# Fixed order for the routing of the last two token tiles in a one-core encoder layer with 16 experts

## The chip, the core and the metric

One core of a Trainium2 chip runs the whole layer in one launch. The metric is the device time of that launch in microseconds (us), lower is better. The core has five instruction streams that run beside each other and wait for each other through semaphores: TensorE (PE in the profile; PEld is its weight load), VectorE (DVE), ScalarE (ACT), GpSimd (POOL) and SyncE (SP), of which the last only issues DMAs here. Each stream runs its own instructions strictly in the order in which the program has them.

## What is computed

512 tokens of width 1024 pass one layer. An input LayerNorm, one combined projection, three mixers beside each other (differential attention, a gated delta rule, a diagonal state-space model) and one output projection give the residual stream, which a second LayerNorm (ln1) normalises. Then comes a mixture of 16 experts and a last LayerNorm. The change stands where ln1 and the routing are:

```python
h = layer_norm(ALPHA * h + mix, ln1_g, ln1_b)
g_prob = softmax(h @ w_grp + b_grp); g_p, g_idx = top_k(g_prob, 1)
e_sel  = the 4 expert logits of that group
e_val, e_idx = top_k(e_sel, 2); e_w = softmax(e_val) * g_p
for e in range(16):
    hid = silu(h @ w1[e]) * (h @ w3[e])
    out += comb[:, e] * (hid @ w2[e])      # comb: 0 unless e was chosen
h = layer_norm(ALPHA * h + out, ln2_g, ln2_b)
```

All is float32; products are split into a high and a low part where needed (`e_hi`, `e_lo`, `w_hi`, `w_lo`).

## The kernel before, in words

**The stage before the experts.** The tokens stand in four tiles of 128. For tile t the generator `out_t(t)` (L1306) is the whole chain from the output projection to the routing: it loads the residual tile `xo`, adds the output projection in three groups of input blocks and two halves of 512 columns (matmuls into `pA`, one VectorE addition each), takes `bn_stats` of the last sum of each half, transposes the half (L1331, four transposes into `pG`, copied to `xT` by ScalarE), computes the 24 router logits from `xT` (`pl`, sixteen small matmuls), finishes the LayerNorm statistics (`ln_end`, a chain of small VectorE operations with Ln and Exp on ScalarE), and forms the logits row `lg` (tile `oblk` in the profile). Then it normalises `xo` with two `scalar_tensor_tensor` operations (L1348 and L1349) and writes it to the arrays `hdr` and `yd` in memory through GpSimd's DMA queue (L1354, L1355). Then the routing proper (L1357 to L1385): `max`, `max_index`, mask, `max`, `max_index`, the two 0/1 rows `o0`, `o1` and their sum `mb`; a small matmul with a triangular matrix counts the tokens ahead (`pr_`) and gives the slot row `sv`. From `sv`, `one_hot` (L212) makes 0/1 matrices `oh` (token by slot) for experts 0 and 1, 2 to 7 and 8 to 15, in three VectorE operations.

**From routing to experts.** The last tile's first `oh` is followed by `slot_rows` (L217): eight tiny matmuls over all four tiles and two small VectorE operations give the table `tab` of the token numbers of experts 0 and 1, which GpSimd needs to gather their tokens from `hdr` into `xg` (L1495). `weights_all` (L1402) computes the gate weights of all tiles into `aux`; `slot_all` (L247) multiplies all `oh` by `aux` with 64 small matmuls (`pS`), and only behind them TensorE's order has `turn_x`, the transposes of the gathered tokens with which expert 0 begins.

**What sets the order.** Instructions inside a `tc.manual_schedule()` block keep the order of the program on each engine. `weights_all`, `slot_all`, and everything of the experts are in such blocks. All before them is ordered by the framework's scheduler: it takes from the program order what it holds to be ready, so the order of `ORDER2` (L37), a list of how many steps of which generator come next, is a priority, and tiles interleave freely on VectorE. The helper `run(g, n)` (L366) advances a generator by n steps.

**The experts.** The weights of 16 experts come in 192 loads of 512 KB (`e_raw`, L1632, on SyncE's queue) into a ring of 32 buffers. The first 28 go as soon as the memory of the earlier stage is free. Load 29 (`FIRST = 28`, L1633) waits by hand for the first two gathers to have landed. Every later load waits for a buffer of the ring, that is for VectorE to have split it or TensorE to have used it. From expert 3 on the order of the experts depends on the token counts (`rank_all`, L255).

Of the kernel before, what the change touches and what calls it, by code (L numbers as in the profile page):

```python
# [15 lines left out]
AF = mybir.ActivationFunctionType  # L16
ALU = mybir.AluOpType
# [4 lines left out]
P = 128  # L22
D = 1024
S = 512
NT = S // P
# [10 lines left out]
          "G11 V1 g2 h G11 S1 G23 G12 S1 V0 G22 S1 G21 V2 G01")  # L36
ORDER2 = ("q00 R3 q01 R1 q10 R4 q11 A01 q20 R1 A02 O11 A01 R1 A02 O01 A03 q21 A01 W2 A11 W2 A01 R1 A11 O01 A12 "  # L37
# [3 lines left out]
NQ4 = 4  # L41
RING = (2, 8, 15, 14, 21, 13, 12, 11, 9, 10, 29, 7, 30, 18, 31, 16, 17, 19, 20, 27, 28, 0, 1, 4, 5, 22, 23, 24, 25, 26, 3, 6)
OHT = 20
# [6 lines left out]
AHEAD = 0  # L50
SW = 12
POOL = 4
NORM = 'vvvv'
KG = ((3, 7, 0, 1), (2, 4, 5), (6,))
FIRST = 28
POOLE = ()
# [23 lines left out]
def tile_layer(ctx: ExitStack, tc: tile.TileContext, a, out):  # L80
    nc = tc.nc

    def tt(o, x, y, op, e=nc.vector):
        return e.tensor_tensor(o, x, y, op=op)  # L84
# [6 lines left out]
    def stt(o, x, s, y, op0, op1):  # L91
        return nc.vector.scalar_tensor_tensor(o, x, s, y, op0=op0, op1=op1)  # L92

    def act(o, x, f, **kw):
        return nc.scalar.activation(o, x, f, **kw)  # L95
# [45 lines left out]
    ident = ones_tile([P, P], "ident")  # L141
# [67 lines left out]
    hdr = dram.tile([S, D], F32, name="hdr")  # L209
    yd = dram.tile([S, D], F32, name="yd_")  # L210
# [6 lines left out]
    def slot_rows(oh, e0, e1, p):  # L217

        p = p[:, 0:2 * (e1 - e0)].rearrange("p (e c) -> p e c", c=2)
        for e in range(e0, e1):  # L220
            for t in range(NT):
                mm(p[:, e - e0], oh[t][e // 8][:, :, e % 8], AXS[t][:, e, 0:2], t == 0, t == NT - 1)
        nc.vector.tensor_reduce(tab[1][:, e0:e1], p, axis=AX.X, op=ALU.add)
        ts(tab[0][:, e0:e1], tab[1][:, e0:e1], 4096.0, ALU.add)
# [133 lines left out]
    gp, ve = nc.gpsimd, nc.vector  # L358
# [7 lines left out]
    def run(g, n=1):  # L366

        for _ in range(n):
            next(g, None)

    with ExitStack() as t1:
        wv = t1.enter_context(tc.tile_pool(name="wv", bufs=1))
# [15 lines left out]
        psA, psG, psT = banks(A=2, G=4, T=2)  # L388

        def per(name, dt=F32, shape=None):  # L390
            return wr.tile(shape or [P, S], dt, name=name, tag="per", bufs=15)
# [50 lines left out]
        for t in range(NT):  # L442
            x = f4("x")
# [3 lines left out]
        for t0 in range(0, NT, LNB):  # L447
# [6 lines left out]
            r = sm.tile([P, LNB], F32, name="ln_rb")  # L454
            rsqrt(r, mv[:, :, 1], LNB, sm, LN_EPS)
            for j in range(LNB):
                x = xs[t0 + j]
# [3 lines left out]
        for k in range(KT):  # L461
            p = psT()
# [17 lines left out]
        beta, g, eg, ek = g6("beta"), g6("g"), g6("eg"), g6("ek")  # L480
# [598 lines left out]
        psA, psG, psT, psV = banks(A=4, G=2, T=1, V=1)  # L1079
# [191 lines left out]
        g1 = []  # L1271
# [27 lines left out]
        MB, OH = [], {}  # L1299
# [3 lines left out]
        TOP = b16[:, 0:64].rearrange("p (t x c) -> p t x c", t=NT, x=2)  # L1303
        O2 = o16.rearrange("p (t x c) -> p t x c", t=NT, x=2)

        def out_t(t):  # L1306
            x = q4k("xo")
            gp.dma_start(x, h0d[t * P:(t + 1) * P, :])
            yield 1
            st_ = sm.tile([P, 2, 6], F32, name="ln_st")  # L1310
            xT = [per("xT"), per("xT")]
            for g_ in KG:
                for n in range(2):
                    c = slice(n * 512, n * 512 + 512)
                    x_ = x[:, c]
                    p = psA()
                    for k in g_:
                        while (k, t) not in yT:
                            run(R if k < 3 else AA[k - 4])
                        while k not in wo:  # L1320
                            run(WO)
                        mm3(p, yT[k, t], [w[:, c] for w in wo[k]], k == g_[0], k == g_[-1])
                    if g_ == KG[0]:
                        stt(x_, x_, ALPHA, p, ALU.mult, ALU.add)
                    else:
                        tt(x_, x_, p, ALU.add)
                    if g_ == KG[-1]:
                        nc.vector.bn_stats(st_[:, n, :], x_)
                        p = psG()
                        for j in range(4):  # L1330
                            nc.tensor.transpose(p[:, j * P:(j + 1) * P], x_[:, j * P:(j + 1) * P], ident)  # L1331
                        act(xT[n], p, AF.Copy)
                    yield 1

            if not g1:
                route_init()
            pl = psG()
            for k in range(KT):
                mm(pl[:, 0:24], xT[k // 4][:, (k % 4) * P:(k % 4 + 1) * P], rw24[:, k, :], k == 0, k == KT - 1)
            mu, r = ln_end(st_, sm)  # L1340
            nmr = sm.tile([P, 1], F32, name="nmr")
            stt(nmr, mu, -1.0, r, ALU.mult, ALU.mult)
            lg = LG[:, t]
            stt(lg, cs24, nmr, rowb, ALU.mult, ALU.add)
            stt(lg, pl[:, 0:24], r, lg, ALU.mult, ALU.add)
            yield 1
            if NORM[t] == "v":
                stt(x, x, mu, g1[0], ALU.subtract, ALU.mult)  # L1348
                stt(x, x, r, g1[1], ALU.mult, ALU.add)  # L1349
            else:  # L1350
                act(x, x, AF.Identity, scale=r, bias=nmr)
                tt(x, x, g1[0], ALU.mult, e=gp if NORM[t] == "p" else ve)
                tt(x, x, g1[1], ALU.add, e=gp)
            gp.dma_start(hdr[t * P:(t + 1) * P, :], x)  # L1354
            gp.dma_start(yd[t * P:(t + 1) * P, :], x)  # L1355
            yield 1
            m8, m8e = TOP[:, t, 0], TOP[:, t, 1]  # L1357
            ix = sm.tile([P, 8], U32, name="ix")
            nc.vector.max(m8, lg[:, 0:8])
            nc.vector.max_index(ix, m8, lg[:, 0:8])  # L1360
            gi = sm.tile([P, 1], F32, name="gi")
            nc.vector.tensor_copy(gi, ix[:, 0:1])
            em = sm.tile([P, 16], F32, name="em")
            ts(em, giq, gi, ALU.not_equal, NEG, ALU.mult)
            tt(em, em, lg[:, 8:24], ALU.add)
            ixe = sm.tile([P, 8], U32, name="ixe")
            nc.vector.max(m8e, em)
            nc.vector.max_index(ixe, m8e, em)
            ei = sm.tile([P, 2], F32, name="ei")
            nc.vector.tensor_copy(ei, ixe[:, 0:2])  # L1370
            o0, o1 = O2[:, t, 0], O2[:, t, 1]
            ts(o0, i16, ei[:, 0:1], ALU.is_equal)
            ts(o1, i16, ei[:, 1:2], ALU.is_equal)
            while len(MB) < t:
                run(OT[len(MB)])
            mb = const.tile([P, 16], BF16, name="mb%d" % t)
            tt(mb, o0, o1, ALU.add)
            MB.append(mb)

            pr_ = psG()  # L1380
            mm(pr_[:, 0:16], oneb, o64, True, False)
            for t_ in range(t):
                mm(pr_[:, 0:16], oneb, MB[t_], False, False)
            mm(pr_[:, 0:16], strib, mb, False, True)
            sv = const.tile([P, 16], BF16, name="sv%d" % t)  # L1385
            stt(sv, mb, -8192.0, pr_[:, 0:16], ALU.mult, ALU.add)
            SV.append(sv)
            yield 1
            oh = [per("oh", BF16, [P, P, 8]) for i in range(2)]
            for i, e0, e1 in ((0, 0, 2), (0, 2, 8), (1, 0, 8)):  # L1390
                one_hot(oh[i][:, :, e0:e1], sv[:, 8 * i + e0:8 * i + e1])
                if t == NT - 1 and e1 == 2:
                    for t_ in range(t):
                        while t_ not in OH:
                            run(OT[t_])
                    OH[t] = oh
                    slot_rows(OH, 0, 2, psT())
            if t < NT - 1:
                OH[t] = oh
            yield 1  # L1400

        def weights_all():  # L1402
# [32 lines left out]
        R, AA, WO = recur(), [attend(i) for i in range(3)], wout()  # L1435
        OT = [out_t(t) for t in range(NT)]
        streams = {"R": R, "W": WO}
        for x in ORDER2.split():
# [9 lines left out]
                run(AA[int(x[1])], int(x[2:]))  # L1448
            else:
                run(streams[x[0]], int(x[1:]))  # L1450
        for x in AA + OT:
            run(x, 20)
        with tc.manual_schedule():
            weights_all()
            pst.close()
            t2 = ctx.enter_context(ExitStack())
            ps2 = t2.enter_context(tc.tile_pool(name="ps2", bufs=1, space=PSUM, reuse_waits="tile"))
            PS = [ps2.tile([P, 512], F32, name="pS", tag="S%d" % i) for i in range(2)]
            CT = PS[1][:, 128:144]
            for t in range(NT):  # L1460
                mm(CT, oneb, MB[t], t == 0, t == NT - 1)
            SA = slot_all(OH, PS[0])
# [8 lines left out]
    def psT():  # L1471
        return ps2.tile([P, 512], F32, name="pT", tag="T", bufs=2)
# [257 lines left out]
    with tc.manual_schedule():  # L1730
# [138 lines left out]
        for x, op in ((0, ALU.mult), (1, ALU.add)):  # L1869
            for c in range(2):  # L1870
                x_ = xs[1][:, half(c)]
# [15 lines left out]
    with tc.If(more > P):  # L1887
        for e in (NE - 2, NE - 1):
            scatter(xgs[e % 2][:, 0:512], at(0, e), 2)
        for r in range(0, S // P):  # L1890
            oh = []
            for t in range(NT):
                p = psT()
# [8 lines left out]
                o = traw().bitcast(BF16).rearrange("p (i s e) -> p i s e", i=2, e=8)  # L1902
# [100 lines left out]
```

## Time and profile before

| | us |
|---|---|
| median of three runs | 780.49 |
| lowest and highest of them | 778.73, 789.08 |
| the profiled execution | 780.58 |
| its span, first to last instruction | 778.8 |
| busy: PE, PEld, DVE, ACT, POOL | 685.2, 497.0, 522.7, 352.5, 101.5 |

The rows further down are from that one profiled execution; their times count from the span's start, and 1.8 us of the execution lie outside the span. A timeline row has the start, the duration, the engine, the line, the operation, its result and inputs, and in brackets the idle time before it with what ended it. A line can be that of a helper: L84 is `tensor_tensor`, L92 `scalar_tensor_tensor`, L95 ScalarE's `activation`, L101 `matmul`.

### The profile page before, as it was taken

How to read it: one execution, taken by the hardware profiler on the slowest of the kernel's cores; microseconds unless marked ns; L12 is line 12 of the kernel's file. 1: busy time of each engine (PE TensorE's matmuls, PEld its weight loads, DVE VectorE, ACT ScalarE, POOL GpSimd, SP SyncE). 2: the span in 40 equal slices, each digit the busy share in tenths (PEclk: the TensorE clock that was granted, in tenths of full speed). 3: DMA queues.
4: the chain of work that ended last, by engine and by line, in shares of the span. 5: the costliest groups of instructions: out<-in, count | busy, mean ns of one | idle time of the engine just before them, and what ended most of it. 6: DMA issues, size and time to landing. Idle time of an engine off the chain costs nothing.

```text
span 778.8 us, 10796 instructions
## 1 busy us (share of the span) xinstructions
PE 685.2 (88%) x3565; PEld 497.0 (64%) x3568; DVE 522.7 (67%) x1368; ACT 352.5 (45%) x572; POOL 101.5 (13%) x138
## 2 busy tenths in 40 slices
PE   0999949997999899999899955989999999999891
PEld 0667737785887676677687745777466577666430
DVE  6999997788662465576756888887267467674316
ACT  2579632723212522254532321766357466764322
POOL 6010000000000011011000012101322212221012
PEclk9999988999878999869689975899999999999996
DMA  6142304120101356436306593899999999999952
GB/s 218 53 136 82 109 0 124 39 60 28 55 4 52 122 149 166 146 77 193 109 28 242 186 399 125 317 365 352 351 382 399 362 377 380 370 362 396 373 213 112
DMA packets 54271, 155.98 MB, mean 200 GB/s; under 512 B 13528, under 2 KB 13784, under 8 KB 54208
## 3 DMA queue, kind: packets, MB, share of 16 engines
q1 hardware_dynamic: 38960, 124.26, 42.4%
q0 software_dynamic: 8192, 19.08, 9.3%
q10 hardware_dynamic: 7056, 11.88, 4.9%
q8 instruction: 30, 0.49, 0.2%
q14 instruction: 33, 0.27, 0.1%
HBM read 139.98 MB, written 19.14 MB: 204 GB/s over the span
## 4 chain that ended last, share of the span: by engine, by line
PE 67%; DVE 15%; DMA 13%; ACT 3%; issue 2%; SPq 0%; DVEq 0%; ACTq 0%
PE pA L101 36%; DMA e_raw<-in_moe_w_dram 12%; PE pG L101 10%; PE pS L101 7%; PE pT L101 4%; PE pV L101 2%; PE po L101 2%; PE pT L1529 1%; PE pT L1225 1%; DVE e_raw L92 1%; DMA x<-in_x_dram 1%; DVE xo L92 1%; DVE e_lo L84 1%; DVE w_lo L84 1%; DMA gb<-in_ln_in_g_dram 1%
## 5 line engine op out<-in xcount | busy, mean ns | idle before, releaser
L84 DVE TENSOR_TENSOR e_lo<-e_raw,e_hi 128x1024 fp32r<-128x1024 f32 x108 | 129.0, 1223 | 33.7 <-ACT e_hi L95 28.6
L95 ACT ACTIVATE e_hi<-e_raw 128x1024 fp32r<-128x1024 f32 x108 | 111.7, 1060 | 30.2 <-DMA e_raw<-in_moe_w_dram 16.4
L101 PE MATMUL pA<-hTh,w_lo 128*128 128x512 f32 x184 | 76.7, 418 | 12.3 <-DVE w_lo L84 12.3
L101 PE MATMUL pA<-hTh,w_hi 128*128 128x512 f32 x184 | 77.9, 423 | 2.5 <-DVE cv L92 1.1
L101 PE MATMUL pA<-hTl,w_hi 128*128 128x512 f32 x184 | 75.1, 409 | 0.0
L101 PE MATMUL pA<-e_hi,xth 128*128 128x512 f32 x144 | 57.7, 401 | 0.3 <-ACT e_hi L95 0.3
L101 PE MATMUL pA<-e_lo,xth 128*128 128x512 f32 x144 | 56.8, 395 | 0.7 <-DVE e_lo L84 0.5
L101 PE MATMUL pA<-e_hi,xtl 128*128 128x512 f32 x144 | 56.6, 393 | 0.0
L101 PE MATMUL pA<-e_raw,xth 128*64 128x512 f32 x224 | 50.3, 595 | 0.0
L101 PEld LDWEIGHTS pA<-hTh,w_lo 128*128 128x128 f32 x184 | 36.3, 197 | 20.5 <-DVE w_lo L84 12.9
L95 ACT ACTIVATE w_hi<-w_raw 128x1024 fp32r<-128x1024 f32 x29 | 30.6, 1055 | 34.9 <-PE pA L101 26.1
L1500 POOL DMA_INDIRECT yd__140<-y,tab x14 | 23.2, 1658 | 175.1 <-ACT y L95 163.3
L101 PEld LDWEIGHTS pA<-hTh,w_hi 128*128 128x128 f32 x184 | 36.1, 196 | 12.6 <-issue 2.1
L101 PEld LDWEIGHTS pA<-hTl,w_hi 128*128 128x128 f32 x184 | 36.0, 196 | 7.7 <-issue 0.7
L84 DVE TENSOR_TENSOR w_lo<-w_raw,w_hi 128x1024 fp32r<-128x1024 f32 x29 | 35.3, 1219 | 2.5 <-ACT w_hi L95 2.4
L84 DVE TENSOR_TENSOR hid<-pA,hid 128x512 f32<-128x512 f32 (+1 forms) x16 | 11.0, 690 | 35.6 <-ACT hid L95 23.1
L101 PEld LDWEIGHTS pA<-e_raw,xth 128*64 128x64 f32 x224 | 15.9, 137 | 29.2 <-issue 27.0
L1495 POOL DMA_INDIRECT xg<-hdr,tab x16 | 30.0, 1872 | 28.0 <-PE pT L1529 8.9
L101 PEld LDWEIGHTS pA<-e_lo,xth 128*128 128x128 f32 x144 | 27.3, 190 | 7.7 <-DVE e_lo L84 2.0
L1206 DVE TENSOR_REDUCE nm<-pA 128x1 f32<-128x128 f32 (+3 forms) x48 | 22.9, 484 | 13.8 <-PE pA L101 9.0
L101 PEld LDWEIGHTS pA<-e_hi,xth 128*128 128x128 f32 x144 | 27.3, 189 | 6.3 <-ACT e_hi L95 0.6
L101 PEld LDWEIGHTS pA<-e_hi,xtl 128*128 128x128 f32 x144 | 27.3, 190 | 5.9 <-DVE xtl L84 0.4
(521 smaller groups left out, 1483.1 us busy)
## 6 DMA issues: line engine op xcount, KB each, us to landing
e_raw<-in_moe_w_dram SPq DMA_DIRECT2D x192, 512.0 KB, 11.3
w_raw<-in_w_cm_dram SPq DMA_DIRECT2D x12, 512.0 KB, 3.3
w_raw<-in_w_cm_dram ACTq DMA_DIRECT2D x11, 512.0 KB, 3.4
qks<-qkd POOLq DMA_DIRECT2D x18, 256.0 KB, 4.0
qkd<-qk SPq DMA_DIRECT2D x6, 512.0 KB, 2.8
h0d<-x SPq DMA_DIRECT2D x4, 512.0 KB, 3.5
w_raw<-in_w_out_dram SPq DMA_DIRECT2D x4, 512.0 KB, 3.8
w_raw<-in_w_out_dram ACTq DMA_DIRECT2D x4, 512.0 KB, 5.6
```

The source lines that it names most:

```text
L84: return e.tensor_tensor(o, x, y, op=op)
L92: return nc.vector.scalar_tensor_tensor(o, x, s, y, op0=op0, op1=op1)
L95: return nc.scalar.activation(o, x, f, **kw)
L101: return nc.tensor.matmul(o, l, r, start=start, stop=stop)
L1206: nc.vector.tensor_reduce(nm[:, c:c + 1], pc[c][:, 0:nk], axis=AX.X, op=ALU.max, negate=True)
L1225: nc.tensor.transpose(pa[:, kb * P:(kb + 1) * P], e[:, kb * P:(kb + 1) * P], ident)
L1495: return nc.gpsimd.indirect_dma_start(out=xg, out_offset=None, in_=rows_of(hdr, n), in_offset=bass.IndirectOffsetOnAxis(ap=idx, axis=0), b ...
L1500: nc.gpsimd.indirect_dma_start(out=rows_of(yd, n), out_offset=bass.IndirectOffsetOnAxis(ap=idx, axis=0), in_=y, in_offset=None, bounds_che ...
L1529: nc.tensor.transpose(p[:, j * P:(j + 1) * P], x[:, j * P:(j + 1) * P], ident)
```

## The change

It has four parts. (1) `ORDER2` ends earlier: tiles 0 and 1 and the attention still run to their end under the scheduler, tile 2 up to its logits and tile 3 up to the second of its three groups. What is left of tiles 2 and 3 moves into the `manual_schedule` block, in an order written out with `bit(t)`, which advances a tile to its next `yield`, the new `yield 0` among them (`run` passes over those). Both halves of tile 3 are transposed together, behind both additions. (2) The norms of tiles 2 and 3 come behind the small operations of tile 3's LayerNorm and ahead of its finished logits. (3) For tiles 2 and 3 the matrices of experts 2 to 15 come behind `slot_rows`; `weights_all` follows them. (4) `NORM = 'vpvv'`: tile 1's norm is one ScalarE operation over 128x1024 and two GpSimd `tensor_tensor` operations over 128x1024.

```diff
@@ ORDER2, its last lines
-          "O12 A22 O21 A21 O31 O11 A21 O21 A21 O03 O31 A22 O11 O01 O21 O11 A22 O01 O13 O21 O02 O21 O11 A21 O31 "
-          "O21 O31 O11 O21 O11 O33 O21 O31 O21 O31 O22")
+          "O12 A22 O21 A21 O31 O11 A21 O21 A21 O03 O31 A22 O11 O01 O21 O11 O01 O21 O11 O02 O12 O21")
-NORM = 'vvvv'
+NORM = 'vpvv'
@@ run
-            next(g, None)
+            while next(g, 1) == 0:
+                pass
@@ new functions, ahead of out_t
+        def turn_out(x, o):
+            p = psG()
+            for j in range(4):
+                nc.tensor.transpose(p[:, j * P:(j + 1) * P], x[:, j * P:(j + 1) * P], ident)
+            act(o, p, AF.Copy)
+
+        NRM = {}
+
+        def norm(t, x, mu, r, nmr):
+            if NORM[t] == "v":
+                stt(x, x, mu, g1[0], ALU.subtract, ALU.mult)
+                stt(x, x, r, g1[1], ALU.mult, ALU.add)
+            else:
+                act(x, x, AF.Identity, scale=r, bias=nmr)
+                tt(x, x, g1[0], ALU.mult, e=gp)
+                tt(x, x, g1[1], ALU.add, e=gp)
+            for o in (hdr, yd):
+                gp.dma_start(o[t * P:(t + 1) * P, :], x)
@@ out_t
                         nc.vector.bn_stats(st_[:, n, :], x_)
-                        p = psG()
-                        for j in range(4):
-                            nc.tensor.transpose(p[:, j * P:(j + 1) * P], x_[:, j * P:(j + 1) * P], ident)
-                        act(xT[n], p, AF.Copy)
+                        if t < NT - 1:
+                            turn_out(x_, xT[n])
+                        elif n:
+                            yield 0
+                            for m in range(2):
+                                turn_out(x[:, m * 512:m * 512 + 512], xT[m])
...
             stt(lg, cs24, nmr, rowb, ALU.mult, ALU.add)
+            NRM[t] = lambda: norm(t, x, mu, r, nmr)
+            yield 0
             stt(lg, pl[:, 0:24], r, lg, ALU.mult, ALU.add)
             yield 1
...
+            if t < 2:
+                NRM[t]()
+                yield 1
...
             MB.append(mb)
+            yield 0
...
             oh = [per("oh", BF16, [P, P, 8]) for i in range(2)]
+            OH[t] = oh
             for i, e0, e1 in ((0, 0, 2), (0, 2, 8), (1, 0, 8)):
                 one_hot(oh[i][:, :, e0:e1], sv[:, 8 * i + e0:8 * i + e1])
...
+                if e1 == 2:
+                    if t == NT - 1:
+                        slot_rows(OH, 0, 2, psT())
+                    yield 0
@@ the end of the stage
-        for x in AA + OT:
+        for x in AA + OT[0:2]:
             run(x, 20)
         with tc.manual_schedule():
+
+            def bit(t):
+                next(OT[t], None)
+
+            bit(2)
+            bit(3)
+            bit(3)
+            bit(2)
+            bit(3)
+            bit(3)
+            bit(2)
+            NRM[2]()
+            NRM[3]()
+            for _ in range(4):
+                bit(3)
+            bit(2)
+            bit(3)
             weights_all()
```

Written out, the block's order is: routing of tile 2 up to `mb`; third group of tile 3, both halves; `sv` of tile 2; transposes of tile 3; its logits matmuls and LayerNorm end; tile 2's first `oh`; norm of tile 2; norm of tile 3; tile 3's logits, routing, `sv`, first `oh` and `slot_rows`; the other `oh` of tile 2, then of tile 3; `weights_all`; `slot_all`.

## Rows read from the trace of the kernel before

**Rows 1.** Busy time by stretch; last three columns: granted clock, DMA share, GB/s.
```profile
core 0: us, PE busy (x) PEld busy (x) DVE busy (x) ACT busy (x) POOL busy (x), PEclk, DMA share, GB/s
...
480.00:490.00 10.00, 5.77 (x80) 5.57 (x80) 7.80 (x35) 1.20 (x3) 2.16 (x2) 0.50 0.16 49
...
680.00:700.00 20.00, 19.10 (x88) 13.10 (x87) 13.54 (x14) 12.66 (x16) 5.50 (x4) 1.00 0.97 359
```
**Rows 2.** Chain that ended last, in order of time: start, us, what.
```profile
484.99 3.97 PE pS L101 x64
488.96 0.97 PE pT L1529 x4
...
668.54 13.65 DMA e_raw<-in_moe_w_dram
```
**Rows 3.** SyncE's wait ahead of load 29: its duration (ns) and start; its releaser.
```profile
L1632 SPq EVENT_SEMAPHORE  x1: 15882/15882/15882, 474.3 to 474.3; - x1
...
SPq L1632 <- DMA xg<-hdr,tab: 15.9, 1, 15.9
```
**Rows 4.** Weight loads, issue to landing: with an empty queue (430.6, 433.0), and at 545.97.
```profile
DMA to landing us min/median/max: 3.1/3.2/3.2
...
DMA to landing us min/median/max: 4.3/4.3/4.3
```
**Rows 5.** VectorE and TensorE busy from 451.03 to the last `sv`, and one stretch of it.
```profile
451.03:481.08 30.05, 16.30 (x88) 13.89 (x86) 26.58 (x120) 5.48 (x17) 5.01 (x8) 0.63 0.76 294
468.28:475.36 7.08, 6.43 (x33) 6.13 (x34) 4.19 (x18) 1.20 (x2) 1.20 (x3) 0.50 0.16 50
```
**Rows 6.** Timeline of VectorE, tile 1's norm to the first table.
```profile
452.77 1.28 DVE L92 SCALAR_TENSOR_TENSOR xo<-xo,ln_mv,g 128x1024 f32<-128x1024 f32 x1
...
455.31 1.26 DVE L92 SCALAR_TENSOR_TENSOR xo<-xo,ln_r,g 128x1024 f32<-128x1024 f32 x1
...
469.70 0.16 DVE L1360 FIND_INDEX8 ix<-b,oblk 128x8 uint32<-128x8 f32 x1
...
469.90 0.15 DVE L1362 CAST gi<-ix 128x1 f32<-128x1 uint32 x1
...
475.36 0.24 DVE L92 SCALAR_TENSOR_TENSOR oblk<-pG,ln_r,oblk 128x24 f32<-128x24 f32 x1 [1.34 <-PE pG L101]
475.52 1.57 DVE L1370 CAST ei<-ixe 128x2 f32<-128x2 uint32 x1
...
478.65 0.54 DVE L84 TENSOR_TENSOR oh<-im,sv 128x768 bf16<-128x768 bf16 x1
...
479.26 0.67 DVE L84 TENSOR_TENSOR oh<-im,sv 128x1024 bf16<-128x1024 bf16 x1
...
479.92 0.16 DVE L84 TENSOR_TENSOR few<-b 128x4 f32<-128x4 f32 x1
479.99 0.16 DVE L1413 TENSOR_REDUCE few<-ge 128x4 f32<-128x16 f32 x1
...
480.91 0.17 DVE L92 SCALAR_TENSOR_TENSOR sv<-mb,pG 128x16 bf16<-128x16 bf16 x1
...
482.14 0.68 DVE L84 TENSOR_TENSOR oh<-im,sv 128x1024 bf16<-128x1024 bf16 x1
482.74 0.16 DVE L88 TENSOR_SCALAR tab<-tab 128x2 int32<-128x2 f32 x1
```
**Rows 7.** Timeline of GpSimd around the first gather.
```profile
475.20 1.86 POOL L1488 MEMSET xg<- 128x1024 f32 x2
483.76 1.10 POOL L1495 DMA_INDIRECT xg<-hdr,tab  x1 [6.70 <-DVE aux L1423]
```
**Rows 8.** GpSimd's `tensor_tensor` over 512 columns: alone, and four beside VectorE.
```profile
746.05 1.27 POOL L84 TENSOR_TENSOR xg<-e_raw 128x512 f32<-128x512 f32 x1 [12.16 <-DVE e_raw L92]
...
763.31 5.50 POOL L84 TENSOR_TENSOR e_raw<-e_raw 128x512 f32<-128x512 f32 x4 [9.29 <-ACT e_raw L95]
```
**Rows 9.** VectorE beside the latter.
```profile
762.83 2.41 DVE L92 SCALAR_TENSOR_TENSOR e_raw<-e_raw,rr 128x512 f32<-128x512 f32 x2
```

More of the change, by code (lines that the diff above doesn't have):

```diff
@@ L1344, in out_t @@
             stt(lg, cs24, nmr, rowb, ALU.mult, ALU.add)
+            NRM[t] = lambda: norm(t, x, mu, r, nmr)
+            yield 0
             stt(lg, pl[:, 0:24], r, lg, ALU.mult, ALU.add)
             yield 1
[L1347 to L1356, printed above, removed]
+            if t < 2:
+                NRM[t]()
+                yield 1
             m8, m8e = TOP[:, t, 0], TOP[:, t, 1]
@@ L1389, in out_t @@
             oh = [per("oh", BF16, [P, P, 8]) for i in range(2)]
+            OH[t] = oh
             for i, e0, e1 in ((0, 0, 2), (0, 2, 8), (1, 0, 8)):
                 one_hot(oh[i][:, :, e0:e1], sv[:, 8 * i + e0:8 * i + e1])
[L1392 to L1399, printed above, removed]
+                if e1 == 2:
+                    if t == NT - 1:
+                        slot_rows(OH, 0, 2, psT())
+                    yield 0
             yield 1
```

## The prediction

> **What bounds the kernel now.** I read the busy time by stretch first. From about 500 us to 720 the DMA engines are full: busy for 0.95 of the time or more in every stretch of 10 or 20 us, for which the one from 680 to 700 with 0.97 stands [rows 1]. Ahead of that lies a hole: between 480 and 490 the DMA share is 0.16 and TensorE has the lower of its two clock levels (0.50 of 2.4 GHz). The chain that ended last says the same. At its end it is made of weight loads (one piece of 13.65 us as the sample); before, it enters the experts through the 64 small matmuls of `slot_all` and the transposes of expert 0 at 488.96 [rows 2]. Then SyncE's waits: ahead of load 29 its queue stands from 474.3 for 15.88 us, to 490.2, until both first gathers have landed [rows 3].
>
> So the end hangs on two dates. One is the gathers' landing, which lets the loads go on (G = 490.2). The other is the start of expert 0's transposes (X = 488.96), because the later loads wait for ring buffers that only the experts' work frees. The time from issue to landing tells which of the two leads: 3.1 us with an empty queue, 4.3 us for the load at 545.97 [rows 4]. That load therefore found only 1.1 to 1.2 us of work ahead of it in the DMA engines. I take it that the loads can bear a later X by 1.1 us and no more. The shift of the end is then the larger of (shift of G) and (shift of X less 1.1). Both dates hang on VectorE, which in the 30.05 us from 451.03 to the last tile's `sv` (its end, 481.08, is called S) is busy for 26.58 us [rows 5].
>
> **Part by part, for S.**
> (a) Tile 1's norm leaves VectorE: 1.28 and 1.26 [rows 6], 2.5 us.
> (b) Tile 2's two later `oh`, 0.54 and 0.67, move behind the table: 1.2 us [rows 6].
> (c) Six small operations of `weights_all` stand between the routings today and come later now. Interleaved small operations start 0.07 us apart (479.92, 479.99), lone dependent ones 0.20 (469.70, 469.90) [rows 6]; six of them, about 0.1 each, 0.6 us.
> (d) Between 468.28 and 475.36 VectorE idles for 7.08 - 4.19 = 2.9 us [rows 5], waiting for transposes and logits of tiles 2 and 3. In the new order the two norms (four operations of about 1.2 us each) stand there, so this idling goes; what is late next is VectorE itself.
> (e) Against it: in a fixed order nothing fills the gaps between dependent operations. The routing of tile 3 has some twelve, its LayerNorm end some ten with a visit to ScalarE: 22 times (0.20 - 0.08), and 0.5 us for ScalarE, 3.1 us. Bounds: 0, if tiles 0 and 1 have left enough work to fill them, and 6.2, if tile 2's routing and the waits for TensorE stand alone too.
> (f) Tile 1's norm arrives on GpSimd: two operations over 1024 columns, by the lone 512-column one (1.27) [rows 8] about 2.5 us each, 5.0 together, in the middle of VectorE's fullest stretch. The trace has one meeting of this kind: beside four such operations two VectorE operations took 2.41 where one of their form at 1024 columns takes 1.28 and two halves should so take about 1.4; and the four took 5.50 instead of 5.08 [rows 8, 9]. So VectorE lost 1.0 us beside one GpSimd operation of 1.27. Bounds: 0 and 5.0. I take the middle, 2.5, since VectorE found room beside the other three.
> ScalarE's own operation for this norm (some 1.1 us) falls where ScalarE has 5.48 us of work in 30 [rows 5]; nothing, and at most 1.1 if tile 3's last input stands behind it. The memory fills that GpSimd does behind the last norm's DMAs hold a VectorE cast for 1.57 us today [rows 6, 7]. They come behind the last norm's DMAs again and meet tile 3's routing; unchanged, at best 1.4 less.
> Sum: -2.5 - 1.2 - 0.6 - 2.9 + 3.1 + 2.5 = -1.6; S = 479.5.
>
> On (f) the Trainium skill goes further than the row. "SBUF — State Buffer", section "SBUF: two separate sides", says that VectorE and GpSimd share a port pair as an exclusive lock: a VectorE operation with two SBUF inputs and a GpSimd operation that reads SBUF exclude each other for a whole instruction. The one meeting agrees as far as it goes, 1.0 us lost. By the rule even the smallest additions of the routing wait, and (f) is 5.0; that is a rival below.
>
> **From S to G.** Today the table is ready at 482.90, 1.82 behind S, with a 0.68 `oh` between its two operations [rows 6]. That one moves away: 1.82 less 0.6, and 0.1 for the dependent step, is 1.3. The gathers then take what they take today, 490.2 - 482.9 = 7.3 us. G = 479.5 + 1.3 + 7.3 = 488.1, a shift of -2.1. The writes of `hdr` are no limit: tile 1's come some 5 us later, far ahead of tile 3's.
>
> **From S to X.** Here the change adds. Behind the table now stand four `oh`, 2 x (0.54 + 0.67) = 2.4, with overlap 2.1. Then the whole of `weights_all`: today 2.1 us pass from the table (482.90) to the start of `slot_all` (484.99) with its first half already done [rows 2, 6]; that half is some five dependent steps of 0.20 and one visit to ScalarE, 1.3. So 2.1 + 2.1 + 1.3 = 5.5 instead of 2.1. Nothing hides it, since `slot_all` needs all `oh` and all of `aux`, and TensorE holds the experts' transposes behind it. `slot_all` itself stays 3.97 at the lower clock [rows 2]. X = 479.5 + 1.3 + 5.5 + 4.0 = 490.3, a shift of +1.3.
>
> **The end.** Gathers: -2.1. Experts: +1.3 - 1.1 = +0.2. The larger is +0.2: 780.58 + 0.2 = 780.8. The sum is made against the profiled execution, which lies 0.1 over the median of 780.49. Everything behind X stays as it is.
>
> **Rivals.**
> *Faster.* The free tiles fill the gaps (e = 0) and GpSimd stays out of the way (f = 0): S = 473.9, X shifts by -4.3, G by -7.7, the end by max(-7.7, -5.4): 775.2. For it: the free part of the order still has two tiles' `oh` to give. Against it: those have higher priority and may be done before the gaps come.
> *Slower.* Tile 1's norm on GpSimd holds VectorE for all of its 5.0 us, from the first two-input operation that meets it at about 455. S = 482.0, X +3.8, the end +2.7: 783.3; with (e) at its upper bound +5.8: 786.4. It decides as soon as VectorE loses over 0.9 us more than I take, since only the gathers have room. For it: the one meeting in rows 8 and 9, and a stretch without other idling. Against: operations with one input from PSUM can go on.
> *The earlier table is worth nothing, and the reserve in the DMA queue too.* Then the end follows X alone: +1.3, 781.9. For it: the reserve rests on one load. Against: later loads wait longer in the queue.
> *The gathers lead.* If the later start of the experts is caught up, as the ring holds 28 loads by then, the end follows G: -2.1, 778.5. Against: the buffers come free by work, not by loads.
>
> **How the numbers follow.** Forecast with the two near cases around it (781.9 and 778.5): 0.55, its own range 778.5 to 783. Faster rival: 0.2. Slower rival: 0.2. The rest, 0.05, is that the scheduler's free part turns out quite differently, since its list was cut. The range takes in the faster and slower cases and 6 us up for those bounds: 775 to 787. Over 2% (15.6 us), about what a measurement of this kernel can tell from no change, none of these comes near: the whole stretch from 451 to X is 38 us, most of it work that stays. I leave 0.03 for faster and 0.05 for slower, where the free part goes wrong, and 0.92 for within 2%.
>
> **What would show it.** Tile 1's norm on GpSimd with VectorE operations drawn out beside it (f); no idling over 1 us behind tile 3's transposes (d); a table 1.3 us behind `sv`; `slot_all` beginning over 5 us behind the table; load 29 ahead of the experts' transposes instead of behind them. If X comes earlier than 487, my sums for (e) or (f) are wrong; if X is later and the end earlier, the 1.1 us are.

## The result and the profile after

| | before | changed |
|---|---|---|
| median, us | 780.86 | 791.0 |
| lowest and highest of four runs | 778.73, 789.08 | 784.36, 795.22 |
| the profiled execution | 780.58 | 789.79 |
| its span | 778.8 | 787.9 |

The changed kernel is slower: ratio 1.0116, 95% interval 1.0071 to 1.0162, some 9 us. That is within the 2% for which the prediction had a chance of 0.92, but outside its range (775 to 787), and beyond its slower rival (783.3, at most 786.4). Executions over 1.5% above the fastest of their kernel are left out of the ratios, and the profiles of c1 and e7 below are of such executions.

The stage begins at another time in each execution: the last `put` of the attention, from which the prediction counted (451.03 before, rows 5), lay between 445.16 and 460.89 in the profiles of this study. So dates are given from it. Ahead of it no loss is to be seen: its median is 449.66 in the nine profiles with the changed order and 451.03 in the five with the old one. S is the end of the last `sv`, as in the prediction. X is the start of expert 0's transposes, counted 0.28 us ahead of the chain's row of them [rows 2], as the expectations count it: 488.68 - 451.03 = 37.65 before.

The chain that ended last of the changed kernel, at the same place as [rows 2], with cuts marked by dots: start, us, what.

```profile
467.04 0.17 DVE mb L83
467.21 0.61 DVE xo L83
467.87 1.13 PE pG L1309 x4
...
470.82 0.60 ACT xT L94
471.42 0.10 ACT rs_y L94
...
474.50 2.49 DVE xo L91 x2
477.02 1.28 DVE xo L91
478.30 0.17 DVE oblk L91
...
479.16 2.39 DVE em L88
...
484.67 0.17 DVE tab L87
484.84 2.13 DVE oh L83 x4
...
490.46 3.96 PE pS L100 x64
494.43 0.97 PE pT L1560 x4
```

From the put at 449.56, S lies at 33.93 (before 30.04) and X at 494.43 - 0.28 - 449.56 = 44.59: 6.94 us later than before. The chain lists where it went: tile 3's first addition (`xo`, 467.21) stands behind tile 2's routing (`mb`), ScalarE's Ln and Exp (`rs_y`) behind both `xT` copies, tile 3's logits (`oblk`, 478.30) behind four norm operations, a 0.2 us step of the routing (`em`) takes 2.39, and behind the table stand four `oh` and the whole weight chain ahead of `slot_all`.

Busy time, same view as [rows 5]; the stretches are put to S, and put to the end of `aux`, the last input of `slot_all` (before: 33.91 long, VectorE busy for 30.12).

```profile
449.56:483.49 33.93, 16.65 (x88) 14.09 (x86) 29.35 (x109) 5.31 (x15) 9.79 (x10) 0.56 0.66 251
449.56:490.41 40.85, 17.24 (x97) 14.65 (x96) 35.01 (x132) 6.57 (x18) 11.98 (x12) 0.55 0.61 229
```

In the second stretch VectorE's busy time grew by 4.89, though two norm operations left it, and its idle time by 2.05 (5.84 instead of 3.79). Busy here includes standing still inside an instruction, as the timelines of VectorE and of GpSimd in the changed kernel show (compare [rows 6, 7]):

```profile
455.21 1.70 DVE L88 TENSOR_SCALAR em<-giq,gi 128x16 f32<-128x16 f32 x1
456.83 0.34 DVE L91 SCALAR_TENSOR_TENSOR yTt<-pT,dngs,yTt 128x128 fp32r<-128x128 f32 x1
457.09 3.45 DVE L83 TENSOR_TENSOR oh<-im,sv 128x256 bf16<-128x256 bf16 x3
...
463.45 1.43 DVE L83 TENSOR_TENSOR oh<-im,sv 128x256 bf16<-128x256 bf16 x3
...
471.77 0.16 DVE L83 TENSOR_TENSOR rs_t<-rs_y 128x1 f32<-128x1 f32 x1 [1.49 <-ACT rs_y L94]
...
479.16 2.38 DVE L88 TENSOR_SCALAR em<-giq,gi 128x16 f32<-128x16 f32 x1
```

```profile
454.53 4.78 POOL L83 TENSOR_TENSOR xo<-xo,g 128x1024 f32<-128x1024 f32 x2 [6.92 <-ACT xo L94]
...
479.12 0.53 POOL L1323 DMA_DIRECT2D yd__140<-xo  x1
479.64 1.86 POOL L1519 MEMSET xg<- 128x1024 f32 x2
485.70 1.17 POOL L1526 DMA_INDIRECT xg<-hdr,tab  x1 [4.20 <-DVE tab L87]
```

`em` of tile 1 (0.23 when alone) lasts 1.70 and ends at 456.91, 0.03 behind the end of the first of the two GpSimd operations (2.35 us long by itself: 454.53 + 2.35 = 456.88). The next three `oh` take 3.45 instead of 1.43. That is 1.47 + 2.02 = 3.5 us. The second `em`, of tile 3, at 479.16 ends at 481.54, when the two zero fills are over (481.50): it is held for 2.2 us. It stands from its start, though the first fill is recorded only 0.48 us later; why is not shown.

Behind X one more thing differs. The chain of before has 48 matmuls `pA` of expert 0 in 10.92 us (first fence); here they take 12.50 (second fence):

```profile
509.12 10.92 PE pA L101 x48
```

```profile
513.91 0.66 PE pT L1560 x4
514.57 12.50 PE pA L100 x48
```

In the stretch from 513.91 to 520.91 the granted clock was 0.76 (first row); in the same stretch of before, from 508.40 to 515.40, it was 1.00 (second fence).

```profile
513.91:520.91 7.00, 7.00 (x26) 5.72 (x27) 3.56 (x4) 3.55 (x4) 0.00 (x0) 0.76 0.83 323
```

```profile
508.40:515.40 7.00, 6.94 (x33) 5.83 (x34) 4.97 (x6) 4.80 (x6) 0.00 (x0) 1.00 0.99 395
```

From the put the end comes 10.6 us later in this profile (338.33 instead of 327.74): 6.9 to X, 1.6 by that fall of the clock, and 2.1 further on. What the 2.1 are made of is not shown; in the second profile of the same kernel (c1, below) they are 1.2.

### The profile page after: what moved, and what is told of

It is laid out like the page before. It is cut to its first block, busy times and chain, and to the rows that moved or that the text cites. A ratio compares the mean times of both kernels' runs of the same rounds, so it can differ in the third digit from the quotient of the medians.

```text
span 787.9 us, 10802 instructions
## 1 busy us (share of the span) xinstructions
PE 688.7 (87%) x3568; PEld 496.3 (63%) x3568; DVE 527.7 (67%) x1366; ACT 353.2 (45%) x573; POOL 106.7 (14%) x140
## 4 chain that ended last, share of the span: by engine, by line
PE 68%; DVE 15%; DMA 12%; ACT 3%; issue 2%; SPq 0%; DVEq 0%
PE pA L100 36%; DMA e_raw<-in_moe_w_dram 11%; PE pG L100 10%; PE pS L100 7%; PE pT L100 4%; PE po L100 2%; PE pV L100 2%; PE pT L1560 1%; DVE e_raw L91 1%; DMA x<-in_x_dram 1%; PE pT L1225 1%; DVE e_lo L83 1%; DVE xo L91 1%; DVE w_lo L83 1%; DMA gb<-in_ln_in_g_dram 1%
## 5 line engine op out<-in xcount | busy, mean ns | idle before, releaser
L100 PEld LDWEIGHTS pA<-hTh,w_lo 128*128 128x128 f32 x184 | 36.4, 198 | 20.6 <-DVE w_lo L83 12.9
L100 PEld LDWEIGHTS pA<-e_raw,xth 128*64 128x64 f32 x224 | 16.2, 137 | 29.5 <-issue 27.1
```

The costliest lines, as they stand in the source:

```text
L100: return nc.tensor.matmul(o, l, r, start=start, stop=stop)
```

## Experiments

The theory that the runs test: the end follows X without any reserve, and X follows what VectorE does, and where it stands still, between put and `aux`. All runs in one table: the ratio is against before with its interval; the times are from each run's profile, S and X from the put, then from X to the issue of the 47th weight load, and from X to the end.

| run | ratio | S | X | X to load 47 | X to end |
|---|---|---|---|---|---|
| before | 1 | 30.04 | 37.65 | 26.71 | 290.08 |
| changed | 1.0116 [1.0071, 1.0162] | 33.93 | 44.59 | 28.28 | 293.74 |
| changed, again (c1) | 1.0135 [1.0090, 1.0180] | 33.95 | 44.62 | 28.30 | 292.83 |
| e7 | 1.0111 [1.0056, 1.0165] | 30.02 | 41.49 | 28.28 | 292.24 |
| e7b | 1.0088 [1.0052, 1.0123] | 30.04 | 41.51 | 28.31 | 291.86 |
| e1 | 1.0106 [1.0078, 1.0135] | 31.99 | 42.65 | 28.44 | 290.91 |
| e2 | 1.0028 [0.9988, 1.0067] | 30.46 | 38.08 | 28.31 | 292.73 |
| e4 | 1.0092 [1.0056, 1.0128] | 31.79 | 42.46 | 28.33 | 291.07 |
| b1 | 1.0020 [0.9993, 1.0048] | 29.13 | 36.85 | 26.70 | 290.33 |
| e5 | 1.0083 [1.0044, 1.0122] | 33.01 | 43.68 | 29.45 | 293.92 |
| e8 | 1.0077 [1.0030, 1.0123] | 32.96 | 43.62 | 29.48 | 293.57 |
| e3 | 1.0062 [1.0023, 1.0101] | 35.00 | 43.98 | 26.70 | 290.06 |
| e9 | 1.0113 [1.0053, 1.0173] | 34.03 | 43.83 | 26.71 | 289.84 |
| e6 | 1.0021 [0.9988, 1.0055] | 27.38 | 37.10 | 29.35 | 291.86 |

X repeats to 0.03 us between executions of one kernel (44.59 and 44.62; 41.49 and 41.51). The whole time does not: its interval is some 3 us to either side. So single edits are judged by X, and the ratio only where it can bear it.

**The changed kernel again (c1).** No edit.

> The changed kernel, unedited, measured beside the others of this batch. Theory (X 6.9 us later behind the put, by work that each execution has; the rest of the 9 us is the granted clock of single executions): X again 44.6 behind the put within 0.2 us; the time 7 to 9 us over before. Rival (the loss is mostly the clock's and changes with the execution): X behind the put varies by over 1 us, or the time is less than 5 us over before.

X came at 44.62 and the time at 792.02, 1.0135 times before, some 10 us over (above the 7 to 9 of the theory). The 6.9 us to X came in both profiled executions; the rival falls.

**Does the end follow X, or has it a reserve? (e7, e7b)** The kernel before with a later X and nothing else:

```diff
-        for e in range(NE):
+        for e in 2 * list(range(NE)):      # slot_all
```

> The kernel before, with the 64 small matmuls of slot_all done twice over: nothing changes ahead of them, the gathers land as before, and X comes 4.0 us later. Theory (the end follows X with no reserve): end about 4 us later, 785, a ratio of 1.005. Rival (the prediction's reserve of 1.1 us in the loads): 2.9 us later. Rival (the gathers' landing at 490.2 leads and X only follows): within 1 us of before.

> The kernel before with the 64 small matmuls of slot_all done twice, once more: the first time the profile had X 3.8 us later behind the put and the end 6.0 us later, of which 1.6 us were a second fall of TensorE's granted clock some 20 us behind X. Theory (the end follows X with no reserve; that fall comes in some executions and not in others): X 3.8 to 4.0 later, time 4 to 6 us over before. Rival (a reserve of 1.1 us): 2.9 us over before or less. Rival (a later X costs more than itself each time): 8 us over before again.

The chain of e7b:

```profile
483.60 7.83 PE pS L101 x128
491.43 0.96 PE pT L1529 x4
```

X came 3.84 and 3.86 later, and the end, from the put, 6.0 and 5.6 later (333.73 and 333.37 against 327.74): all of X's shift, 1.6 by the clock behind X, and a rest of 0.6 and 0.2. Nothing is left of the 1.1 us that the prediction held back. The table says the same without any sum: in the four profiles whose clock does not fall behind X (before, b1, e3, e9; X to load 47 of 26.7) the end lies 289.84 to 290.33 behind X, while X itself goes from 36.85 to 43.98. The gathers were where they were before (load 29 at 39.21 and 39.04 from the put, before 39.16), so they don't lead. By the whole times the shift is 8.7 us [4.4, 12.9] and 6.9 us [4.1, 9.6]: at least X's.

**GpSimd beside VectorE (e1, e2).** e1 takes tile 1's norm back to VectorE in the changed kernel; e2 does that part of the change alone, in the kernel before.

```diff
-NORM = 'vpvv'      # e1, in the changed kernel
+NORM = 'vvvv'
-NORM = 'vvvv'      # e2, in the kernel before
+NORM = 'vpvv'
```

> The changed kernel with tile 1's norm back on VectorE (NORM = 'vvvv'), all else as changed. Theory A (the end follows X, the start of expert 0's transposes, and X is what VectorE's waiting makes it): the 3.5 us for which VectorE stood behind GpSimd's two operations go, the norm's 2.4 us come back, X comes about 1 us earlier than the 494.4 of the changed kernel (493 to 494). Rival B (the GpSimd norm is hidden, the fixed order alone costs the time): X comes 2.4 us later, about 496.8.

> The kernel before with tile 1's norm on ScalarE and GpSimd alone (NORM = 'vpvv'), order and matrices as before. Theory A: VectorE loses 3 to 4 us behind GpSimd and saves 2.5, X at 489 to 490.5 instead of 488.96, the end within 2 us of before. Rival C (the GpSimd norm is most of the loss): X at 492 or later, the end 4 us or more later.

In e1 X comes 1.94 earlier (some 1 was expected), although VectorE has 2.54 us more to do. In e2 it comes 0.43 later. The timelines of VectorE and GpSimd in e2 show the mechanism most clearly:

```profile
454.78 2.16 DVE L89 TENSOR_SCALAR em<-giq,gi 128x16 f32<-128x16 f32 x1
456.86 0.34 DVE L92 SCALAR_TENSOR_TENSOR yTt<-pT,dngs,yTt 128x128 fp32r<-128x128 f32 x1
457.12 2.27 DVE L84 TENSOR_TENSOR em<-em,oblk 128x16 f32<-128x16 f32 x1
```

```profile
454.57 4.79 POOL L84 TENSOR_TENSOR xo<-xo,g 128x1024 f32<-128x1024 f32 x2 [6.93 <-ACT xo L95]
```

Two operations over 16 columns, 0.23 and 0.16 when alone, last until the GpSimd operation beside each of them ends (456.94 and 456.92; 459.39 and 459.36, the two being 2.35 and 2.36 us long from 454.57 and 456.99). `yTt`, with one input from PSUM, takes its 0.34 between them. VectorE loses 4.0 us. The Trainium skill ("SBUF — State Buffer", section "SBUF: two separate sides") states it so: the port pair that the two engines share is an exclusive lock, for a VectorE operation in a two-port mode as for one with two SBUF inputs against a GpSimd operation that reads SBUF, and whichever starts first has it for the whole instruction. The trace agrees, to 0.03 us; in which mode the first `em` runs, it does not show. In the kernel before, the norm's 2.54 paid for most of the loss, and VectorE's idle time up to S fell by 0.6 (2.82 of 30.46 us, before 3.47); in the fixed order the norm on GpSimd costs 1.9 net.

**The zero fills (e4, b1).** The same edit in the changed kernel and in the one before:

```diff
     for x in xgs:
-        nc.gpsimd.memset(x, 0.0)
+        act(x, onec.to_broadcast([P, D]), AF.Copy, scale=0.0)
```

> The changed kernel with the two zero fills of xg (128x1024 each) on ScalarE instead of GpSimd. Theory A: the 2.38 us of tile 3's mask operation fall to 0.2 to 0.3, S, the table and X come 2.1 us earlier (X 492.3), the end about 2 us earlier. Rival E (GpSimd's DMA issues hold VectorE, not the fills): the mask operation still takes over 1 us and X moves by less than 1 us.

> The kernel before, with the two zero fills of xg as ScalarE operations instead of GpSimd MEMSETs. Theory (a fill on GpSimd stalls VectorE in the kernel before as well, by 1.4 us): the cast beside the fills falls from 1.57 us to about 0.15, the time from the last put to expert 0's transposes (X) falls from 37.65 to about 36.2, and the end follows X: about 779.4 us, 0.998 of before. Rival (the fills cost nothing in the kernel before, because VectorE waits for other engines in this stretch anyway): X stays at 37.5 or more behind the put, time unchanged.

X comes 2.13 earlier in the changed kernel, as expected, and 0.80 in the one before, where 1.4 were expected. The held operations are short now; first `em` in e4, then the cast in b1, 1.57 in [rows 6]:

```profile
474.76 0.23 DVE L88 TENSOR_SCALAR em<-giq,gi 128x16 f32<-128x16 f32 x1
```

```profile
477.69 0.16 DVE L1370 CAST ei<-ixe 128x2 f32<-128x2 uint32 x1
```

The rival, GpSimd's DMA issues, falls too. The write to `yd` starts 0.04 us ahead of `em` in the changed kernel (479.12, above) and in e4, and in e4 `em` takes its 0.23 beside it:

```profile
474.73 0.53 POOL L1323 DMA_DIRECT2D yd__140<-xo  x1
```

So the same two fills cost 1.3 us more in the changed kernel. The hold itself is 0.7 longer there, 2.2 instead of 1.4, and it meets a later step of a chain with nothing beside it. The whole time of b1 shows no gain; 0.8 us is below what it can show.

**The order (e5, e8).** e5 puts tile 3's third group and its transposes ahead of tile 2's routing; e8 puts tile 3's Ln and Exp ahead of its transposes, and so of ScalarE's `xT` copies.

```diff
-            bit(2)             # e5
             bit(3)
             bit(3)
+            bit(3)
+            bit(2)
             bit(2)
             bit(3)
-            bit(3)
             bit(2)
```

```diff
                         elif n:             # e8; ln_end's second half stays where it was
+                            mv = sm.tile([P, 2], F32, name="ln_mv")
+                            nc.vector.bn_aggr(mv, st_.rearrange("p a b -> p (a b)"))
+                            vy = rsqrt_1(mv[:, 1:2], 1, sm, LN_EPS)
                             yield 0
...
```

> The changed kernel, with one move in the hand-written order: tile 3's third group and its transposes come ahead of tile 2's routing. Theory (some 4 us of the loss come from the order itself: tile 2's routing keeps tile 3's additions back, and VectorE later idles behind the transposes): tile 3's additions and transposes start about 2.4 us earlier relative to the put, X falls from 44.6 to about 42 behind the put, time about 788.5. Rival (VectorE is bound by the sum of its work, and an order cannot change that): X stays within 1 us of 44.6.

> The changed kernel; tile 3's statistics, with their Ln and Exp, are emitted ahead of its transposes, so that in ScalarE's order they come ahead of the xT copies. Theory (VectorE's 1.5 us of idling behind tile 3's transposes, which wait for ScalarE's Exp behind the xT copies, are on the path): that wait goes, the norms and all behind them come 1.0 to 1.5 us earlier, X about 43.3 behind the put instead of 44.6, time about 789.5. Rival (what is late next is the logits' matmuls, or the two norms that start earlier only meet another wait): X stays within 0.5 us of 44.6.

e5 gains 0.91, e8 0.97; of the 2.6 and 1.3 us expected, less than half and three quarters. In e8 the wait for Exp shrinks from 1.49 to 0.43:

```profile
471.23 0.16 DVE L83 TENSOR_TENSOR rs_t<-rs_y 128x1 f32<-128x1 f32 x1 [0.43 <-ACT rs_y L94]
```

In e5 tile 3's first addition comes 5.2 us earlier from the put (462.00 - 449.66 = 12.34 instead of 467.13 - 449.56 = 17.57), but the first norm operation only 0.91 (472.38 - 449.66 = 22.72 instead of 473.19 - 449.56 = 23.63): tile 2's routing, until then ahead of the additions, now stands between them and tile 3's statistics, and VectorE has to do it either way. That much of the rival, VectorE's sum of work, was right; its own sign, X within 1 us of 44.6, came true by 0.1 us.

**Behind the table (e3, e9).** e3 forms all matrices of tiles 2 and 3 ahead of `slot_rows`; e9 puts the first four operations of the weights into tile 3's routing, and one `oh` of tile 2 where VectorE waits for `slot_rows`.

```diff
-                if e1 == 2:                             # e3
-                    if t == NT - 1:
-                        slot_rows(OH, 0, 2, psT())
-                    yield 0
+            if t == NT - 1:
+                slot_rows(OH, 0, 2, psT())
+            yield 0
```

```diff
+            if t == NT - 1:                             # e9, behind the second max
+                weights_1()
...
-                        slot_rows(OH, 0, 2, psT())
+                        slot_rows(OH, 0, 2, psT(), lambda: next(OT[2], None))
...
```

> The changed kernel with all matrices of tiles 2 and 3 ahead of slot_rows, so the first table comes behind them. Theory A: the work ahead of slot_all is the same, X stays at 494.4 within 0.7, load 29 (492.0 in the changed kernel) goes out about 2 us later, the end does not move. Rival D (the end follows the gathers' landing): the end is 2 us later than in the changed kernel.

> The changed kernel; the two differences and two Exps of the gate weights stand inside tile 3's routing, and one matrix of tile 2 where VectorE waits for the eight matmuls of slot_rows. Theory (behind the table VectorE's order alone delays slot_all, and these five operations fit into gaps that a fixed order otherwise leaves open): about 0.2 us are added ahead of the last sv, about 1.2 us go behind the table; X about 43.6 behind the put, time about 790. Rival (no gap is left that takes them, so what is taken away behind the table comes back ahead of it): X within 0.4 us of 44.6.

In e3 load 29 went 1.6 us later than in the changed kernel (44.02 from the put instead of 42.42), and X came 0.61 earlier. Its time is 1.0062 of before where the changed kernel's is 1.0116 and 1.0135. The intervals overlap, so the times alone only speak against an end 2 us later; but from X the end comes as in before (290.06 and 290.08), though load 29 went 4.9 us later than there. The end goes with X, not with the gathers. e9 has X 0.76 earlier; 0.1 was added ahead of S, and 0.87 less stood between the table and `slot_all`.

**All together (e6).** The edits of e1, e4, e5, e8 and e9 in one kernel.

> The changed kernel with every cause taken out that the runs so far point to: all norms on VectorE; zero fills on ScalarE; tile 3's third group and transposes ahead of tile 2's routing; tile 3's Ln and Exp ahead of its xT copies in ScalarE's order; the first four operations of the gate weights inside tile 3's routing; one matrix of tile 2 placed where VectorE waits for slot_rows. Theory (the end follows X, X follows VectorE's work and stalls): X about 37 to 38 behind the put, time about 781, equal to before; load 29 then goes ahead of X. Rival (the fixed order loses because a fixed order as such leaves gaps that only the scheduler fills): X stays above 40, time above 784. Rival (something behind X is slower in the changed kernel): X about 37.5 but time 785 or more.

Busy time of e6, put to S and put to the end of `aux`; then the latter in b1:

```profile
454.64:482.02 27.38, 14.54 (x88) 12.52 (x86) 25.40 (x113) 5.79 (x18) 3.16 (x6) 0.64 0.72 269
454.64:488.01 33.37, 15.13 (x97) 13.08 (x96) 30.80 (x134) 7.47 (x19) 4.85 (x8) 0.62 0.70 262
```

```profile
452.70:485.81 33.11, 17.49 (x97) 14.94 (x96) 28.95 (x134) 7.56 (x19) 4.30 (x7) 0.56 0.68 264
```

X is at 37.10, where the changed kernel has 44.59: the five edits take back 7.5 us, all of the loss (one by one they gave 6.7, so they do not quite add up). The time is 1.0021 [0.9988, 1.0055], not to be told from before; the expected equality holds. The first rival falls by X; of the second (785 or more) the interval leaves the edge, 785.4. Load 29 did not go ahead of X (37.90 from the put): the first gather starts 2.6 us behind the table (486.01, table 483.37) instead of 0.9 as in the changed kernel. Whether it waits there for tile 3's rows in `hdr`, whose write was issued at 479.20, was not tried. The comparison with b1 says why there is no gain either. Both have the same 134 VectorE operations and no fill in their way. The fixed order leaves VectorE idle for 2.57 us, the scheduler's for 4.16; but the same operations are busy for 30.80 instead of 28.95. Their single durations add up to the same (37.7 and 37.8), so they overlap less: small dependent operations stand one behind the other instead of between others. No kernel of this study is shown to beat before.

## Why the prediction was wrong

**What bounds the kernel: right in the date, wrong in the reserve.** X governs. The step "the loads can bear a later X by 1.1 us" failed: it was read from one load's time from issue to landing [rows 4], and e7 and e7b show X's whole shift at the end. That is 1.1 us of the miss. The rival in which the gathers lead falls by e7, where X alone moved and the end with it, and by e3.

**S to the table, to the gathers, to X: right.** Predicted 1.3, 5.5 and 4.0; measured 1.35, 484.84 to 490.46 = 5.6, and 3.96. The table to load 29 took 7.1 (predicted 7.3), and load 29 (491.98) does go ahead of the transposes (494.43), as foretold.

**S itself: predicted -1.6, measured +3.89.** Nearly all of X's miss, 5.5 of 5.6 us, is here, in three terms. The first two are each the difference that one run made, the third is what is left.

1. *(a) and (f), the norm on GpSimd: predicted -2.5 + 2.5 = 0, measured +1.9 (e1).* The mechanism was right, (f) was too small. VectorE was held for 3.5 us here and 4.0 in e2, between the 2.5 taken and the 5.0 of the rival. The step that failed was to take the middle between 0 and 5.0 "since VectorE found room beside the other three" [rows 8, 9]. What VectorE had at hand there were operations with an input from PSUM, the kind that passed in e2; these rows of the kernel before follow the one in [rows 9]:

```profile
765.16 1.40 DVE L92 SCALAR_TENSOR_TENSOR e_raw<-pT,nm,e_raw 128x512 f32<-128x512 f32 x2
766.48 1.28 DVE L1812 BATCH_NORM_STATS2 st<-pA 128x6 f32<-128x512 f32 x2
```

The price to take was the whole duration of each GpSimd operation, less what has run of it when the first VectorE operation that it holds arrives: here the first had run for 0.7 of its 2.35 us when `em` came, and `em` lost 1.5. e1 gains 0.7 of its 1.9 in VectorE's idle time, behind the hold (5.84 to 5.15).

2. *The zero fills: predicted unchanged, measured +1.2 at S (33.93 - 31.79 = 2.14 in e4, less 30.04 - 29.13 = 0.91 in b1).* The text saw that they would meet tile 3's routing, and took the old price for it. In the scheduler's order a hold of 1.4 cost 0.9 at S; in the fixed chain, with nothing to go beside it, a hold of 2.2 cost 2.1.

3. *(b) to (e), the order: predicted -1.2 - 0.6 - 2.9 + 3.1 = -1.6, left by subtraction +0.7, a miss of 2.3.* The step that failed is (d): the two norms "stand there, so this idling goes". They stand behind tile 3's Exp, and that behind ScalarE's copies: VectorE idles for 1.49 first (e8: 0.97 of it on the path). And tile 2's routing stands ahead of tile 3's additions instead of beside them (e5: 0.91). Some 0.4 of the 2.3 was not tried by itself. That as much could be had, by another order than the change's, is shown by e6 against b1: S is 1.75 earlier. That this is close to the -1.6 of (b) to (e) is no proof of those four terms, which no run took apart.

**The end.** 5.5 at S, 0.1 behind it and 1.1 of reserve make X's part of the miss; the rest, 10.6 - 6.9 in the profile, is TensorE's clock (1.6) and what comes after it (2.1, unexplained), for which the prediction had no term: "everything behind X stays as it is" failed too. The slower rival named the right cause with S + 0.9, but stayed too low (783.3, and 786.4 with (e) at its bound): it left the fills, the reserve and the clock as they were. Its condition, that it decides only from 0.9 us of loss on, does not follow from the prediction's own sum, in which X leads the gathers already (+0.2 against -2.1).

The sum had it in its numbers, but did not say it: with X as the governing date, work moved from ahead of the table to behind it is worth nothing, since X waits for both. (b) and (c) took 1.8 us off S, and the stretch from the table to `slot_all` grew from 2.1 to 5.5. e6 shows it: S 1.75 earlier than in b1, X 0.25 later.

## What to carry to other kernels

Ask which date the end hangs on, and count an edit's work up to that date, not up to the nearer one that it makes earlier. An operation given to GpSimd beside a busy VectorE should be priced at its whole duration there, until a run shows less (here VectorE lost 3.5 and 4.0 of 4.7 us); a stall costs most in a fixed chain, where nothing else stands ready. Where single executions differ by more than the effect, measure from an event just ahead of the change: X repeated to 0.03 us where the whole time scattered by several.

## What was not expected of the hardware

**A MEMSET on GpSimd holds VectorE too**, although it reads nothing: a cast over two columns for 1.4 us more [rows 6], `em` over 16 columns for 2.2. With the fills on ScalarE both took their 0.16 and 0.23 (b1, e4). The two fills took 1.86 us on GpSimd and 1.99 on ScalarE.

**TensorE's clock behind X comes in a few fixed patterns.** The time from X to the 47th weight load took three values in 14 profiles: 26.7 (before, b1, e3, e9), 28.3 to 28.4 (seven profiles) and 29.4 to 29.5 (e5, e6, e8). Before expert 0's `hid` transposes TensorE stands idle for 3.2 to 3.3 us in all 14. What differs is the granted clock. Where the time is 26.7, it rises from 0.50 to 1.00 (2.4 GHz) at 4.4 to 4.8 us behind X and stays there. In five of the seven it rises at 3.8 to 4.1 and falls to 0.50 just behind that idle time, for some 3 us; in e5, e6 and e8 it rises at 4.9 to 5.2 and falls in the last us of the idle time, for some 7. In the last two, e1 and e4, it rises only at 9.3 and 9.6 and does not fall. So in these profiles the same idle time was followed by a fall or not, and the date of the rise tells which. The two kernels that were profiled twice had the same value twice (changed 28.28 and 28.30, e7 28.28 and 28.31); two pairs do not show that a kernel always keeps its value. Which edit leads to which value was not foreseeable from these runs; it is 1.6 or 2.7 us, as much as one of the edits themselves.
